# Two-layer diffusion block: adaLN vectors from VectorE to TensorE, beside layer 0's up products

## The chip, the cores and the metric

One core of a Trainium2 chip. The metric is the device time in microseconds of one launch of the whole program, here the median of several runs. All arithmetic is float32, or pairs of reduced-precision float32 parts (below).

## The reference

Two layers work on 256 context tokens and 1024 latent tokens of width 1024. Each layer computes six adaLN vectors, a token mixer and a ConvFFN. Cut to what matters:

```python
def adaln(cv, w, b):
    m = jax.nn.silu(cv) @ w + b                 # cv: (1024,), w: (1024, 6*1024)
    return 6 vectors of 1024: shift, scale, gate of the mixer; shift, scale, gate of the FFN

for i in range(2):
    sh1, sc1, ga1, sh2, sc2, ga2 = adaln(c, w_mod[i], b_mod[i])             # latent tokens
    csh1, csc1, cga1, csh2, csc2, cga2 = adaln(c_ctx, w_mod[i], b_mod[i])   # context tokens
    a = rms_norm(h, g_mix[i]) * (1 + sc1) + sh1
    h = h + ga1 * mixer_i(a)          # layer 0: Fourier mixing and gated linear attention; layer 1: attention
    f = rms_norm(h, g_ffn[i]) * (1 + sc2) + sh2
    h = h + ga2 * conv_ffn(f)         # (silu(conv(f @ w_up)) * ...) @ w_down, width 2 x 2816
```

In layer 1 the context tokens end after the key and value projections, so only its first two vectors (shift and scale of the mixer) are needed for both conditions; the other four are needed for the latent tokens alone.

## The kernel before

Large products run on TensorE in three passes (`mm3`, line 517 on): both operands are split into a high and a low part, and three of the four partial products are summed. Splits are one cast on ScalarE and one subtraction on VectorE or GpSimd (`split`, L207 and L203). All weights and stored activations are loaded by SyncE's queue in the order in which the scheduler puts them.

Both FFN products use a seven-product scheme of block sums. An *up product* of layer 0 is one of seven per half step: 12 matmuls of 320 columns for one 128-wide pair of columns f and one half of the tokens (`up_step`, `PRODS`). There are 22 values of f and two halves: 44 half steps, 308 products. Their results are evacuated by ScalarE (L1306, L1308, L1312, L1316) and added on VectorE, then go through a convolution (`up_conv`, L1332 to L1344) and are stored to `y_d` (L1351). The up weights are loaded by L1216 in pieces of 512 KB, two for each f, and split ahead of time as buffers come free (`Ups`). Seven *down products* follow (`DOWN`, L1460 on: weights loaded by L1447 and L1453, y by L1390). Each has four row blocks of 11 x 2 x 3 matmuls of 320 columns (256 in layer 1). Eleven tiles of y have to be summed and split before each of them (`Ys`); a tile is made when a buffer of `S` is idle, so most of the next product's tiles come while the last row block of the present one runs. L917 adds the results into the residual.

adaLN before is worked on VectorE, apart from the first two vectors of layer 0 (`adaln_pe` has one of them on TensorE). The generator `cond` (L326 to L341) takes a vector in four column quarters of 256. For each quarter and each of eight row chunks k it loads 128 x 256 weights on SyncE's queue (L331, three or five buffers in turn), and multiplies and adds them into an accumulator with one instruction per condition (`nv`): L335 for k = 0, L337 for the others. A 32 x 32 transpose (L340) and a reduction (L341) follow, and at the end of the vector four small matmuls against `sel` (`cond_end`) sum over partitions; each of the four writes its own strip of 32 PSUM partitions. It is called in three places:

- layer 0's vectors 2 to 5, two conditions, in the mixing stage at low priority (lines 986 to 992);
- layer 1's vectors 0 to 3 as the generator `bg` of layer 0's `ffn`, one step at every second f of the down products (L1537 on);
- layer 1's vectors 4 and 5 in the q/k/v stage, two steps for each token chunk (`tok_chunk`, `MODN`).

```python
for v in range(nv):
    a, s = acc[:, v * n:(v + 1) * n], scv[:, k, v:v + 1]
    if k == 0:
        behind(V.tensor_scalar_mul(a, r, s))
    else:
        behind(V.scalar_tensor_tensor(a, r, s, a, ALU.mult, ALU.add))
```

The order on each engine comes from a scheduler that works through the program by priorities; on TensorE, in the FFN, the order is that of the program. Each engine and SyncE's queue then runs its instructions in that order.

Of the kernel before, what the change touches and what calls it, by code (L numbers as in the profile page):

```python
# [20 lines left out]
P = 128  # L21
D = 1024
# [82 lines left out]
def tile_hybrid_dit(  # L105
# [54 lines left out]
    make_identity(nc, ident)  # L160
    V.memset(ones, 1.0)
    V.memset(onesd, 1.0 / D)
    V.tensor_reduce(sel, ident.rearrange("p (q i) -> p i q", i=32), AX.X, ALU.add)
# [83 lines left out]
    with tc.manual_schedule(engines={mybir.EngineType.Activation}):  # L247
        A.activation(scv.rearrange("p k v -> p v k"), vecs[:, 0:16].rearrange("p (v k) -> p v k", v=2), AF.Silu)
        A.preload_act_table_set("natural_log_exp_and_others")
# [24 lines left out]
    def adaln_pe(m, j, raw):  # L274

        ps = psum[:, XB[0] * 512:(XB[0] + 1) * 512]
        for k in range(KT):
            PE.matmul(ps[:2, 0:256], scv[:, k, :], raw[k // 4][:, k % 4, :], start=k == 0, stop=k == KT - 1)
        free(*raw)
        st = SM(256)  # L280
        A.copy(st[:2], ps[:2, 0:256])
        for i in range(2):
            PE.transpose(ps[:, 256 + 2 * i:258 + 2 * i], st[:2, i * P:(i + 1) * P], ident[:2, :2])
        adaln_add(m, j, ps[:, 256:260])

    def adaln_dve(m, j, raw):

        acc = W((2, 256))
        for k in range(KT):
            for v in range(2):  # L290
                if k == 0:
                    V.tensor_scalar_mul(acc[:, v, :], raw[0][:, 0, :], scv[:, 0, v:v + 1])
                else:
                    V.scalar_tensor_tensor(acc[:, v, :], raw[k // 4][:, k % 4, :], scv[:, k, v:v + 1], acc[:, v, :],
                                           ALU.mult, ALU.add)
# [26 lines left out]
    def cond(l, m, nv, n, acc, raw, R, t=None, after=None):  # L322
# [4 lines left out]
        for q in range(D // n):  # L327
            for k in range(KT):
# [3 lines left out]
                for v in range(nv):  # L332
                    a, s = acc[:, v * n:(v + 1) * n], scv[:, k, v:v + 1]
                    if k == 0:
# [651 lines left out]
    with stream(6):  # L986
        ta, tr = AM(1280), AM(1280)
        R = ta[:, 1024:1280].rearrange("p (m v b) -> p m v b", m=4, v=2)
        for m in (2, 3, 4, 5):
            run(cond(0, m, 2, 256, ta[:, 0:512], tr.a, R[:, m - 2], ta[:, 512:1024], start[:, 0:1] if m == 2 else None))  # L990
        cond_end(0, 2, 6, 2, R, XB)
        free(ta, tr)
# [366 lines left out]
    LEAVE = (4, 4, 4, 5, 2, 2, 0)  # L1359
    BGM = 2  # L1360
    AHEAD = 3
# [105 lines left out]

    def ffn(l, n, ups, ops, side, bg, y_d, h_d, after, sides, nsingle, tail, last_groups):

# [10 lines left out]
        for i, (f, hfs) in enumerate(visits):  # L1480
            up = ups.need(i, "A11")
            for hf in hfs:
# [4 lines left out]
                def freed(a, b):  # L1487
# [8 lines left out]
                step = up_step(l, n, hf, f, lambda a: ups.need(i, a), ops[hf], (0, 5) if i < nsingle + 1 else (0, 8) if i < len(visits) - 1 else (0, 4), CU, freed)  # L1496
                while True:
                    try:
# [9 lines left out]
        run(done)  # L1508
        ux.free()
        run(side)  # L1510
# [91 lines left out]
        run(sides)  # L1602
        run(bg)

    def adaln_l1(ms):

        t = S(1280)
        R = halo.rearrange("p f j i -> p (f j i)")
        due = iter(())
        for m in ms:  # L1610
            nv = 2 if m < 2 else 1
            r = R[:, 0:nv * 32].rearrange("p (m v b) -> p m v b", m=1, v=nv)
            for i, _ in enumerate(cond(1, m, nv, 256, t[:, 0:512], t[:, 512:1280], r[:, 0])):
                if i == LATE:
                    next(due, None)
                yield
            due = adaln_end(m, nv, r)
        for _ in range(LATE):
            yield
        next(due, None)  # L1620
        t.free()

    def adaln_end(m, nv, r):
        cond_end(1, m, m + 1, nv, r, (3, 1))
        if m in (1, 4):
            make_gain(1, m // 4)
        yield

    LATE = 6
    h_d = dr.tile([D, TOK], F32, name="h_d")  # L1630
# [100 lines left out]
    with stream(7), tc.manual_schedule(engines={mybir.EngineType.PE}):  # L1731
        def later(): 
            yield from att_side(n_att[0])
        ffn(0, HALF, ups, ops, ffn_side(f_norm[1], ops[1], 1), adaln_l1((0, 1, 2, 3)), y_d, h_d, ffn0_after, later(), 3, a_gen,
            [(r, (0, 1)) for r in range(4)])
# [5 lines left out]

    MODN = 2
    mod_gen = iter(())
# [60 lines left out]
    with stream(8):  # L1804
# [52 lines left out]
        run(a_gen)  # L1857
        mod_gen = adaln_l1((4, 5))
        k_s, v_s = [], []
# [17 lines left out]
    with stream(9.5):  # L1877
        vv(1, v_w())
        free(*a_t[1])
        run(mod_gen)  # L1880

# [246 lines left out]
```

## Time and profile before

| | us |
|---|---|
| three timed runs | 3147.92, 3154.57, 3156.55 (median 3154.57) |
| the profiled execution, and its span | 3148.77, 3147.0 |
| TensorE, VectorE, ScalarE, GpSimd busy | 2786.3, 2548.2, 1446.5, 1529.9 |
| granted clock of TensorE, mean | 0.935 of full |

In the timeline, layer 0's up products run from 713 to 1306 us and its down products to 1690; the q/k/v stage of layer 1 follows. Layer 1's up products run from 2342 to 2860, its down products to 3137. adaLN's L335 and L337 stand from 39 to 331 us (layer 0) and from 1315 to 1806 (layer 1).

How to read it: a line of a group gives program line, engine, operation, tiles, shape and count, then busy us and mean ns of one, then the idle time of the engine ahead of it and what ended that. Lines of waits give who waited for whom: us in total, times, longest. L203 and L207 are helpers (`tt`, `split`) that many stages use; L154 is every matmul.

### The profile page before, as it was taken

What the parts mean: (1) busy time and instruction counts of PE and PEld (TensorE: products, weight loads), DVE (VectorE), ACT (ScalarE), POOL (GpSimd) and SP (SyncE); (2) the same over time, 40 slices, a digit from 0 to 9 for tenths busy, and PEclk for the clock granted to TensorE, in tenths of its full rate; (3) what the DMA queues carried; (4) which work ended last, traced back from release to release, by engine and by line L of the source; (5) the groups of instructions that cost most, each with busy time, mean ns of one, the idle gap of its engine ahead of it and who ended that gap; (6) DMA issues with size and microseconds to landing.
All of it is one profiled execution on the core that took longest, in us unless ns stands there. A gap on an engine that the chain in (4) does not pass through costs nothing.

```text
span 3147.0 us, 52185 instructions
## 1 busy us (share of the span) xinstructions
PE 2786.3 (89%) x19633; PEld 2681.6 (85%) x19633; DVE 2548.2 (81%) x4103; ACT 1446.5 (46%) x2882; POOL 1529.9 (49%) x1229
## 2 busy tenths in 40 slices
PE   6999988987999999976889799999977999888788
PEld 4898977987999999965879788989967899888788
DVE  6899589878778877899987988867768788787774
ACT  3543444545444544422252446756645455454333
POOL 2024284046554444466753563343377665554661
PEclk7999989998999999987899899999988999998899
DMA  8554302421222222696645420030132222228763
GB/s 271 179 171 133 108 31 93 139 100 47 75 72 75 68 77 66 209 282 192 215 137 188 139 82 20 14 97 28 51 99 62 78 76 77 71 65 273 232 218 107
DMA packets 399984, 371.28 MB, mean 118 GB/s; under 512 B 18267, under 2 KB 336371, under 8 KB 399732
## 3 DMA queue, kind: packets, MB, share of 16 engines
q1 hardware_dynamic: 398674, 365.89, 36.8%
q8 instruction: 154, 2.52, 0.3%
q10 hardware_dynamic: 1058, 2.07, 0.2%
q14 instruction: 98, 0.80, 0.1%
HBM read 282.95 MB, written 84.93 MB: 117 GB/s over the span
## 4 chain that ended last, share of the span: by engine, by line
PE 20%; DVE 16%; DMA 5%; issue 5%; ACT 4%; POOL 2%; SPq 0%; DVEq 0%; ACTq 0%; POOLq 0%
PE psum L154 19%; DVE t L203 7%; POOL t L203 2%; DVE t L337 2%; PE psum L158 2%; DMA t<-in_w_ffn_down_dram 1%; DVE t L1777 1%; DMA t<-in_w_mod_dram 1%; ACT t L1332 1%; ACT t L207 1%; DMA t<-in_w_att_out_dram 1%; DVE t L917 1%; DVE ring L203 1%; DVE t L1338 1%; DVE t L1342 1%
## 5 line engine op out<-in xcount | busy, mean ns | idle before, releaser
L154 PE MATMUL psum<-t,t 128*128 128x256 f32 (+3 forms) x17896 | 2614.5, 307 | 280.4 <-DVE t L203 121.4
L154 PEld LDWEIGHTS psum<-t,t 128*128 128x128 f32 x17896 | 2499.0, 197 | 350.4 <-DVE t L203 132.5
L203 POOL TENSOR_TENSOR t<-t,t 128x512 fp32r<-128x512 f32 (+9 forms) x736 | 1068.9, 1467 | 908.7 <-ACT t L207 577.9
L203 DVE TENSOR_TENSOR t<-t,t 128x512 fp32r<-128x512 f32 (+14 forms) x760 | 784.8, 1060 | 146.5 <-ACT t L207 108.9
L207 ACT CAST t<-t 128x512 fp32r<-128x512 f32 (+5 forms) x857 | 555.9, 670 | 706.3 <-POOL t L203 162.9
L203 POOL TENSOR_TENSOR t<-t 128x512 f32<-128x512 f32 (+3 forms) x265 | 328.3, 1255 | 453.1 <-ACT t L663 155.0
L203 DVE TENSOR_TENSOR t<-t,psum 128x320 f32<-128x320 f32 (+4 forms) x416 | 202.1, 506 | 55.8 <-PE psum L154 44.0
L1332 ACT ACTIVATE t<-t,cvs 128x639 f32<-128x639 f32 (+3 forms) x176 | 153.0, 870 | 146.5 <-DVE t L203 137.3
L337 DVE SCALAR_TENSOR_TENSOR t<-t,scv 128x256 f32<-128x256 f32 x224 | 172.8, 797 | 31.1 <-DMA t<-in_w_mod_dram 29.4
L207 ACT CAST t<-psum 128x512 fp32r<-128x512 f32 (+3 forms) x248 | 130.6, 536 | 135.2 <-PE psum L154 57.5
L1926 POOL TENSOR_SCALAR t<-t,ring 128x640 f32<-128x640 f32 x128 | 101.3, 803 | 169.5 <-DVE ring L1916 80.2
L203 DVE TENSOR_TENSOR t<-psum,t 128x512 fp32r<-128x512 f32 (+3 forms) x248 | 151.2, 615 | 35.5 <-ACT t L207 32.7
L158 PE MATMUL psum<-ident,t 128*128 128x128 f32 (+2 forms) x955 | 152.9, 281 | 28.9 <-DVE t L203 17.8
L158 PEld LDWEIGHTS psum<-ident,t 128*128 128x128 f32 (+2 forms) x955 | 113.5, 144 | 38.5 <-DVE t L203 23.3
L1915 DVE TENSOR_REDUCE ring<-psum 128x1 f32<-128x640 f32 x128 | 104.5, 818 | 18.9 <-PE psum L154 13.1
L917 DVE SCALAR_TENSOR_TENSOR t<-psum,mods,t 128x256 f32<-128x256 f32 (+2 forms) x208 | 92.6, 474 | 28.0 <-PE psum L154 26.7
L337 DVE SCALAR_TENSOR_TENSOR t<-t,scv,t 128x256 f32<-128x256 f32 x224 | 112.9, 555 | 2.4 <-DMA t<-in_w_mod_dram 2.1
L1917 ACT ACTIVATE t<-psum,ring 128x640 f32<-128x640 f32 x128 | 102.2, 799 | 21.8 <-DVE ring L1923 9.8
L1337 DVE SCALAR_TENSOR_TENSOR t<-t,cvs 128x641 f32<-128x641 f32 (+1 forms) x44 | 65.0, 1478 | 49.0 <-ACT t L1332 49.0
L1334 ACT ACTIVATE t<-t 128x511 f32<-128x511 f32 (+3 forms) x88 | 60.4, 686 | 75.2 <-DVE t L1338 45.6
L1344 DVE SCALAR_TENSOR_TENSOR t<-t,cvs 128x255 f32<-128x255 f32 (+1 forms) x66 | 90.2, 1390 | 0.6
L1342 DVE SCALAR_TENSOR_TENSOR t<-t,cvs,t 128x255 f32<-128x255 f32 (+1 forms) x66 | 62.4, 971 | 34.9 <-ACT t L1332 34.9
(145 smaller groups left out, 1688.5 us busy)
## 6 DMA issues: line engine op xcount, KB each, us to landing
t<-in_w_ffn_up_dram SPq DMA_DIRECT2D x98, 512.0 KB, 4.1
t<-in_w_mod_dram SPq DMA_DIRECT2D x320, 128.0 KB, 2.6
t<-in_w_ffn_down_dram SPq DMA_DIRECT2D x96, 256.0 KB, 4.3
t<-in_w_even_in_dram SPq DMA_DIRECT2D x28, 512.0 KB, 4.5
t<-in_w_ffn_down_dram SPq DMA_DIRECT2D x72, 192.0 KB, 3.3
t<-y_d SPq DMA_DIRECT2D x20, 640.0 KB, 7.3
t<-in_w_ffn_down_dram SPq DMA_DIRECT2D x24, 512.0 KB, 4.2
t<-in_w_qkv_dram SPq DMA_DIRECT2D x24, 512.0 KB, 4.7
```

What stands on the lines that cost most here:

```text
L154: cls.keep(out_, nc.tensor.matmul(out_, *args, **kw).ins)
L158: cls.keep(out_, nc.tensor.transpose(out_, *args).ins)
L203: return (eng or V).tensor_tensor(out_, a, b, op)
L207: A.copy(hi, src)
L337: behind(V.scalar_tensor_tensor(a, r, s, a, ALU.mult, ALU.add))
L917: last_resid[0] = V.scalar_tensor_tensor(h[:, n % 2, a:b], ps[:, a - c0:b - c0], mods[:, l, m, n, v:v + 1], h[:, n % 2, a:b], ALU.mult, AL ...
L1332: A.activation(x, c[:, j, at:at + m], AF.Identity, bias=tap(l, 3, ft), scale=tap(l, 1, ft))
L1342: V.scalar_tensor_tensor(x[:, s0 + 1:e], c[:, j, 2 + s0:1 + e], tap(l, 0, ft), x[:, s0 + 1:e], ALU.mult, ALU.add)
L1344: i = V.scalar_tensor_tensor(x[:, s0:s1 - 1], c[:, j, 3 + s0:2 + s1], tap(l, 2, ft), x[:, s0:s1 - 1], ALU.mult, ALU.add)
L1915: V.tensor_reduce(mx[:, i:i + 1], ps, AX.XY, ALU.max)
L1917: A.activation(pt[:, i * HALF:(i + 1) * HALF].rearrange("p (b n) -> p b n", b=2), ps, AF.Exp, bias=nb[:, i:i + 1], scale=SCALE, accum_out= ...
L1926: G.tensor_scalar(pt[:, i * HALF:(i + 1) * HALF], pt[:, i * HALF:(i + 1) * HALF], ex[:, i:i + 1], 1.0, ALU.mult, ALU.mult)
```

## The change

Seven vectors leave VectorE: all six of layer 1, and layer 0's last one (5, the gate of the down product). `cond` and `cond_end` stay for layer 0's vectors 2 to 4. The new generator `cond_up` is stepped once after each up product of layer 0, from the second half of the fourth f on. It holds PSUM bank 7 for itself; the up products then turn through seven banks instead of eight. For each of eight chunks k it loads 128 full rows of a vector (512 KB, one buffer in `ring`) and, four products later, issues four float32 matmuls. Their stationary operand is 32 columns of `scv` (the first two are the two conditions; `scv` is padded with zeros for that), the moving one is a column quarter of 256, and each quarter's sums go to its own strip of 32 partitions. The next row's load is issued behind them. After the eighth chunk the sums are copied to SBUF in two pieces (ScalarE); each piece is transposed on TensorE two products after its copy, and one VectorE instruction adds the bias. Both conditions are computed for every vector.

```diff
-    scv = gp.tile([P, KT, 2], F32, name="scv")
+    scv = gp.tile([P, 2 * KT + 32], F32, name="scv")
...
-        for m in (2, 3, 4, 5):
+        for m in (2, 3, 4):
...
-(0, 5) if i < nsingle + 1 else (0, 8) if i < len(visits) - 1 else (0, 4), CU, freed)
+(0, 5) if i < nsingle + 1 else (0, 7) if i < len(visits) - 1 else (0, 4), CU, freed)
...
+                    if hf or i > nsingle:
+                        next(beside, None)
...
-                    if f % BGM:
-                        next(bg, None)
...
+    def cond_up(vecs_lm, bank):
+        ps = psum[:, bank * 512:(bank + 1) * 512]
+        raw, st = ring[:, 0:D], ring[:, D:D + P]
+        for l, m in vecs_lm:
+            for k in range(KT):
+                DMA(raw, w_mod[l, k * P:(k + 1) * P, m * D:(m + 1) * D])
+                for _ in range(COND_LATE):
+                    yield
+                for g in range(4):
+                    PE.matmul(ps[g * 32:(g + 1) * 32, 0:256], scv[:, 2 * k:2 * k + 32], raw[:, g * 256:(g + 1) * 256],
+                              start=k == 0, stop=k == KT - 1)
+            for i in range(2):
+                A.copy(st, ps[:, i * P:(i + 1) * P])
+                yield
+                yield
+                PE.transpose(ps[:, 256 + i * P:256 + (i + 1) * P], st, ident)
+            sums = ps[:, 256:512].rearrange("p (i g q) -> p g i q", i=2, q=32)[:, :, :, 0:2]
+            tt(mods[:, l, m].rearrange("p (g i) v -> p g i v", i=2), sums,
+               bmod(l, m).rearrange("p (g i) v -> p g i v", i=2), ALU.add)
+            if l and m in (1, 4):
+                make_gain(1, m // 4)
+    COND_LATE = 4
...
-        ffn(0, ..., adaln_l1((0, 1, 2, 3)), ...)
+        ffn(0, ..., cond_up([(1, 0), (1, 1), (0, 5)] + [(1, m) for m in (2, 3, 4, 5)], 7), ...)
...
-        for _ in range(MODN):
-            next(mod_gen, None)
...
-        mod_gen = adaln_l1((4, 5))
...
-        run(mod_gen)
```

The order on TensorE in the middle of layer 0's up products, before: two rows of six matmuls are one product (the names are the weight tile and the tile of the tokens' operand).

```order
L154 MATMUL psum<-t_6132,t_8528 128x320 x6
L154 MATMUL psum<-t_6135,t_8528 128x320 x6
L154 MATMUL psum<-t_6172,t_8546 128x320 x6
L154 MATMUL psum<-t_6252,t_8546 128x320 x6
L154 MATMUL psum<-t_6167,t_8549 128x320 x6
L154 MATMUL psum<-t_6247,t_8549 128x320 x6
```

The same engine at such a place now, from one group of adaLN matmuls to the next:

```order
L154 MATMUL psum<-ring,scv 32x256 x4
L154 MATMUL psum<-t_6602,t_9078 128x320 x6
L154 MATMUL psum<-t_6680,t_9078 128x320 x6
L154 MATMUL psum<-t_6641,t_9081 128x320 x6
L154 MATMUL psum<-t_6739,t_9081 128x320 x6
L154 MATMUL psum<-t_6660,t_9101 128x320 x6
L154 MATMUL psum<-t_6720,t_9101 128x320 x6
L154 MATMUL psum<-t_5904,t_9274 128x320 x6
L154 MATMUL psum<-t_5951,t_9274 128x320 x6
L154 MATMUL psum<-ring,scv 32x256 x4
```

Four float32 matmuls of 256 columns stand between every fourth and fifth product, 56 times, and two transposes after each eighth time.

VectorE in layer 0's down products, between the second and the third of them, before (t of 128 x 640 are splits of y, of 128 x 1280 sums of y; `ring,mods` are residual adds):

```order
L917 SCALAR_TENSOR_TENSOR t_12503<-ring,mods,t_12503 128x320
L203 TENSOR_TENSOR t_12737<-t_11759,t_12737 128x640
L337 SCALAR_TENSOR_TENSOR t_11815<-t_11815,scv 128x256 x2
L203 TENSOR_TENSOR t_12765<-t_11759,t_12765 128x640
L203 TENSOR_TENSOR t_11786<-t_12681,t_11786 128x1280
L203 TENSOR_TENSOR mods<-psum,vecs 128x16
L337 SCALAR_TENSOR_TENSOR t_11815<-t_11815,scv 128x256 x4
L203 TENSOR_TENSOR t_12853<-t_11786,t_12853 128x640
```

And now, at the same seam:

```order
L918 SCALAR_TENSOR_TENSOR t_12629<-ring,mods,t_12629 128x320
L204 TENSOR_TENSOR t_12837<-t_11973,t_12837 128x640
L204 TENSOR_TENSOR t_12000<-t_12778,t_12000 128x1280
L204 TENSOR_TENSOR t_12869<-t_12000,t_12869 128x640
L204 TENSOR_TENSOR t_12317<-t_12799,t_12317 128x640
L204 TENSOR_TENSOR t_12873<-t_12317,t_12873 128x640
```

The adaLN instructions between splits, sums and adds are gone; nothing stands in their place. (The changed program's lines lie one higher from line 162 on.)

SyncE's queue in the middle of the up products, before, over two values of f:

```order
L1216 DMA t_10991<-in_w_ffn_up_dram 128x8x128
L1216 DMA t_10975<-in_w_ffn_up_dram 128x8x128
L1351 DMA y_d<-t_6310 128x641
L1351 DMA y_d<-t_6310 128x639
L1216 DMA t_11231<-in_w_ffn_up_dram 128x8x128
L1216 DMA t_11215<-in_w_ffn_up_dram 128x8x128
```

And now:

```order
L1217 DMA t_10410<-in_w_ffn_up_dram 128x8x128
L1217 DMA t_10394<-in_w_ffn_up_dram 128x8x128
L1611 DMA ring<-in_w_mod_dram 128x1024
L1352 DMA y_d<-t_6207 128x641
L1611 DMA ring<-in_w_mod_dram 128x1024 x2
L1352 DMA y_d<-t_6207 128x639
L1217 DMA t_10665<-in_w_ffn_up_dram 128x8x128
L1611 DMA ring<-in_w_mod_dram 128x1024
L1217 DMA t_10649<-in_w_ffn_up_dram 128x8x128
```

The rows of adaLN weights stand among the up weights and the stores of y, some right behind both up loads of an f, some between them.

More of the change, by code (lines that the diff above doesn't have):

```diff
@@ L161, in tile_hybrid_dit @@
     V.memset(ones, 1.0)
+    V.memset(scv, 0.0)
     V.memset(onesd, 1.0 / D)
@@ L247, in tile_hybrid_dit @@
     with tc.manual_schedule(engines={mybir.EngineType.Activation}):
-        A.activation(scv.rearrange("p k v -> p v k"), vecs[:, 0:16].rearrange("p (v k) -> p v k", v=2), AF.Silu)
+        A.activation(scv[:, 0:2 * KT].rearrange("p (k v) -> p v k", v=2), vecs[:, 0:16].rearrange("p (v k) -> p v k", v=2), AF.Silu)
         A.preload_act_table_set("natural_log_exp_and_others")
@@ L277, in adaln_pe @@
         for k in range(KT):
-            PE.matmul(ps[:2, 0:256], scv[:, k, :], raw[k // 4][:, k % 4, :], start=k == 0, stop=k == KT - 1)
+            PE.matmul(ps[:2, 0:256], scv[:, 2 * k:2 * k + 2], raw[k // 4][:, k % 4, :], start=k == 0, stop=k == KT - 1)
         free(*raw)
@@ L291, in adaln_dve @@
                 if k == 0:
-                    V.tensor_scalar_mul(acc[:, v, :], raw[0][:, 0, :], scv[:, 0, v:v + 1])
+                    V.tensor_scalar_mul(acc[:, v, :], raw[0][:, 0, :], scv[:, v:v + 1])
                 else:
-                    V.scalar_tensor_tensor(acc[:, v, :], raw[k // 4][:, k % 4, :], scv[:, k, v:v + 1], acc[:, v, :],
+                    V.scalar_tensor_tensor(acc[:, v, :], raw[k // 4][:, k % 4, :], scv[:, 2 * k + v:2 * k + v + 1], acc[:, v, :],
                                            ALU.mult, ALU.add)
@@ L332, in cond @@
                 for v in range(nv):
-                    a, s = acc[:, v * n:(v + 1) * n], scv[:, k, v:v + 1]
+                    a, s = acc[:, v * n:(v + 1) * n], scv[:, 2 * k + v:2 * k + v + 1]
                     if k == 0:
@@ L1359, in tile_hybrid_dit @@
     LEAVE = (4, 4, 4, 5, 2, 2, 0)
-    BGM = 2
     AHEAD = 3
@@ L1466, in tile_hybrid_dit, with ffn @@
     WE = ((G, G, G), (V, G, V))
-    def ffn(l, n, ups, ops, side, bg, y_d, h_d, after, sides, nsingle, tail, last_groups):
+    def ffn(l, n, ups, ops, side, beside, y_d, h_d, after, sides, nsingle, tail, last_groups):
         u = n // 2
@@ L1495, in freed @@
                         pump(w_gen, (W, 1))
-                step = up_step(l, n, hf, f, lambda a: ups.need(i, a), ops[hf], (0, 5) if i < nsingle + 1 else (0, 8) if i < len(visits) - 1 else (0, 4), CU, freed)
+                step = up_step(l, n, hf, f, lambda a: ups.need(i, a), ops[hf], (0, 5) if i < nsingle + 1 else (0, 7) if i < len(visits) - 1 else (0, 4), CU, freed)
                 while True:
@@ L1508, in ffn @@
         run(done)
+        run(beside)
         ux.free()
@@ L1602, in ffn @@
         run(sides)
[L1603 to L1615, printed above, removed]
-                yield
[L1617 to L1629, printed above, removed]
+    def cond_up(vecs_lm, bank):
[11 more added lines that the diff above has]
+                A.copy(st, ps[:, i * P:(i + 1) * P])
+                yield
+                yield
[6 more added lines that the diff above has]
+    COND_LATE = 4
     h_d = dr.tile([D, TOK], F32, name="h_d")
@@ L1733, in later @@
             yield from att_side(n_att[0])
-        ffn(0, HALF, ups, ops, ffn_side(f_norm[1], ops[1], 1), adaln_l1((0, 1, 2, 3)), y_d, h_d, ffn0_after, later(), 3, a_gen,
+        ffn(0, HALF, ups, ops, ffn_side(f_norm[1], ops[1], 1), cond_up([(1, 0), (1, 1), (0, 5)] + [(1, m) for m in (2, 3, 4, 5)], 7), y_d, h_d, ffn0_after, later(), 3, a_gen,
             [(r, (0, 1)) for r in range(4)])
```

6 lines of the change are left out of this document (2 added, 4 removed).

## The prediction

> **What bounds the kernel now.** I read the stages first. These windows are layer 0's up products (two parts: start and steady run), its down products, the first part of layer 1's q/k/v stage, and layer 1's down products. The borders come from the timeline: the last evacuation of an up product and the last residual add of a stage. Columns: us, then busy us (instructions) of each engine, granted clock, DMA share, GB/s.
>
> ```profile
> 713.00:830.00 117.00, 96.66 (x569) 94.11 (x568) 96.51 (x116) 62.26 (x104) 74.83 (x52) 0.87 0.19 58
> 830.00:1260.00 430.00, 425.97 (x2895) 424.77 (x2895) 344.32 (x433) 211.94 (x370) 211.17 (x183) 1.00 0.23 72
> 1306.00:1690.00 384.00, 306.74 (x1880) 296.04 (x1879) 356.66 (x467) 118.11 (x197) 230.05 (x155) 0.88 0.69 214
> 1690.00:1860.00 170.00, 138.77 (x1063) 133.16 (x1061) 149.10 (x317) 74.01 (x238) 95.53 (x87) 0.91 0.37 114
> 2860.00:3137.00 277.00, 243.84 (x1911) 238.69 (x1910) 190.35 (x279) 95.94 (x179) 140.53 (x97) 0.92 0.66 207
> ```
>
> The steady up run is TensorE's: 425.97 of 430 us busy at full clock. Whatever TensorE is given there lengthens the span one for one. Layer 0's down stage is VectorE's: 356.66 of 384 us, while TensorE has 306.74 and a clock of 0.88. In layer 1's down stage, which has no adaLN beside it, VectorE is busy 190.35 of 277 us.
>
> What does TensorE need there by itself? The code gives 7 products x 4 row blocks x 11 x 2 halves x 3 = 1848 matmuls per down stage. The next two windows lie in runs without a gap, of 320 columns (layer 0) and of 256 (layer 1):
>
> ```profile
> 1000.00:1100.00 100.00, 100.00 (x683) 100.00 (x682) 80.64 (x101) 49.05 (x86) 46.66 (x42) 1.00 0.22 69
> 2966.00:2986.00 20.00, 20.00 (x171) 20.00 (x170) 10.72 (x15) 5.88 (x11) 12.21 (x10) 1.00 0.74 220
> ```
>
> So one matmul takes 0.146 us at 320 columns and 0.117 us at 256. Layer 0's down stage needs 1848 x 0.146 = 270 us and takes 384: it loses 114. Layer 1's needs 216 us, and some 7 for the 64 final transposes (at 0.11 us, an estimate from the 0.216 us per 256 float32 columns found below), and takes 277: it loses 54.
>
> Who makes TensorE wait in layer 0's down stage, who holds the DMA queue, and what the chain of waits goes through (three views of 1306 to 1690):
>
> ```profile
> PE psum L154 <- DVE t L203: 51.9, 18, 10.0
> PE psum L154 <- ACT t L207: 11.3, 7, 5.8
> PE psum L154 <- POOL t L203: 7.2, 4, 2.6
> SPq L331 <- DVE t L337: 98.5, 82, 4.8
> SPq L331 <- DVE t L335: 30.4, 17, 5.8
> by line: DVE t L203 13.0%; DVE t L337 9.9%; DMA t<-in_w_mod_dram 8.3%; issue 6.5%; DVE t L917 4.5%; DMA t<-in_w_ffn_down_dram 1.1%; DMA t<-sd 1.0%; DVE t L335 1.0%; DVE ring L340 0.7%; ACT t L207 0.5%; SPq L331 0.5%; POOL t L203 0.3%; DVE h
> ```
>
> TensorE waits for VectorE's splits of y, at the seams between products. VectorE has adaLN instructions (L335, L337) between those splits, and SyncE's queue stands 129 us behind them with its next adaLN row, so that weight and y loads behind it come late too. adaLN's own part of the chain is 9.9 + 8.3 + 1.0 + 0.7 + 0.5 = 20.4% of 384 = 78 us.
>
> **The change, part by part.**
>
> *Down stage, layer 0: removed.* adaLN's instructions there:
>
> ```profile
> L337 DVE SCALAR_TENSOR_TENSOR t<-t,scv 128x256 f32<-128x256 f32 x176 | 136.7, 809 | 19.3 <-DMA t<-in_w_mod_dram 18.3
> L335 DVE TENSOR_SCALAR t<-t,scv 128x256 f32<-128x256 f32 x26 | 18.1, 722 | 1.2 <-DMA t<-in_w_mod_dram 1.1
> L340 DVE STREAM_TRANSPOSE ring<-t 128x512 f32<-128x512 f32 (+1 forms) x16 | 9.2, 574 | 0.3
> L341 DVE TENSOR_REDUCE halo<-ring 128x16 f32<-128x512 f32 (+1 forms) x15 | 8.4, 558 | 0.4
> ```
>
> That is 172 of VectorE's 357 busy us, and all L331 transfers with their queue waits. What remains is late next: the y splits, sums and residual adds of VectorE (185 us), GpSimd's splits (230 us), TensorE's 270. Three prices for the gain. Low: adaLN's share of VectorE, 172/357, of the 52 us for which TensorE sat behind it: 25 us. Nearest row: layer 1's loss of 54 us, scaled by 320/256 since y is wider, is 67; 114 - 67 = 47 us. High: adaLN's part of the chain, 78 us. I take 52: layer 1 is the nearest, and it carries weight splits on VectorE that layer 0 leaves to GpSimd. The freed buffer (one more y tile made ahead) is within that.
>
> *q/k/v stage: removed.* Two vectors with one condition each:
>
> ```profile
> L337 DVE SCALAR_TENSOR_TENSOR t<-t,scv 128x256 f32<-128x256 f32 x48 | 36.2, 754 | 11.8 <-DMA t<-in_w_mod_dram 11.2
> L335 DVE TENSOR_SCALAR t<-t,scv 128x256 f32<-128x256 f32 x6 | 4.0, 672 | 0.0
> PE psum L158 <- DVE t L203: 15.7, 6, 5.2
> PE psum L154 <- DVE halo L341: 5.2, 1, 5.2
> by line: DVE t L1777 19.1%; DVE t L203 17.4%; PE psum L154 15.0%; issue 14.8%; DVE t L337 9.2%; DVE ring L203 5.2%; DMA t<-in_w_qkv_dram 4.8%; DMA t<-in_w_mod_dram 3.7%; DVE ring L1123 1.8%; DVE t L335 1.6%; DVE ring L340 1.2%; DVE ring L38
> ```
>
> The chain carries 9.2 + 3.7 + 1.6 + 1.2 = 15.7% of 170 = 27 us of adaLN. TensorE's waits behind VectorE are 21 us, of which the 5.2 for adaLN's own reduction surely goes, and of the others adaLN's 40 of 149 busy us: 9 us. Between 9 and 27 I take 17.
>
> *Mixing stage: removed.* A quarter of the vectors there (one of four, two conditions):
>
> ```profile
> L337 DVE SCALAR_TENSOR_TENSOR t<-t,scv,t 128x256 f32<-128x256 f32 x202 | 103.0, 563 | 1.4 <-DMA t<-in_w_mod_dram 1.3
> PE psum L154 <- DVE t L203: 21.6, 17, 3.1
> PE psum L154 <- DVE cvs L238: 5.1, 2, 4.3
> ```
>
> 56 of L337's instructions at 0.563 are 32 us of VectorE, between 100 and 350 us. TensorE waits for VectorE only later (350 to 720: the last two rows), 27 us. The scheduler also orders the GLA and Fourier work anew, which can cost as well as gain. I take a gain of 6, between -8 and 20.
>
> *Up stage, layer 0: added.* 7 vectors x 8 chunks = 56 bursts of four float32 matmuls of 256 columns, to four strips of 32 partitions. No row has such a burst. One strip alone (8 matmuls, two passes each) is in the first row; then four strips at 8, 16 and 64 columns. At 8 columns, 1640.18 starts the first pass and 1640.24 the second, with the products before and after beside them; at 16 and 64 columns the two rows are the two passes:
>
> ```profile
> 75.79 3.62 PE L154 MATMUL psum<-t,scv 128*2 128x256 f32 x16
> 1639.94 0.31 PE L154 MATMUL psum<-t,t 128*128 128x320 f32 x1
> 1640.18 0.25 PE L154 MATMUL psum<-halo,sel 128*32 128x8 f32 x8
> 1640.62 0.60 PE L154 MATMUL psum<-t,t 128*128 128x320 f32 x3
> 1640.24 0.19 PE L154 MATMUL psum<-halo,sel 128*32 128x8 f32 x3
> 1527.30 0.20 PE L154 MATMUL psum<-halo,sel 128*32 128x16 f32 x1
> 1527.35 0.21 PE L154 MATMUL psum<-halo,sel 128*32 128x16 f32 x4
> 406.97 0.30 PE L154 MATMUL psum<-t,sel 128*32 128x64 f32 x4
> 407.07 0.31 PE L154 MATMUL psum<-t,sel 128*32 128x64 f32 x4
> ```
>
> A pass of 256 columns in one strip takes about 3.46/16 = 0.216 us (3.62 less the last one's tail). The 8-column burst cost the stream of products 1640.62 - 1639.94 - 2 x 0.146 = 0.39 us, with a pass of 0.05 to 0.06. At 16 columns a pass is still 0.05, at 64 it is 0.10: twice what one strip of 64 would take by the first row (64 x 0.216/256 = 0.054). If four strips run fully beside each other, a burst is 0.39 + 2 x (0.216 - 0.055) = 0.71 us, 40 us for all. If the 0.10 grows with the columns, a pass is 0.40 and a burst 1.08, 60 us. One after another: eight passes of 0.216 and the switching, about 2.0 us, 112 in all. The 64-column row is nearest in size, so I take 1.0: 56 us. The 14 transposes are 128 columns each with a switch: an estimate from the same row is 0.11 for the columns and as much for the gap: 3 us. The copies, the seven adds and the gains lie beside products on engines with room (ScalarE 212, VectorE 344 of 430 us). One PSUM bank fewer costs nothing: a half step uses four, and seven still leave each one nearly a whole step before its next use.
>
> *New waits.* One row buffer: after a burst the next 512 KB row has four products, 48 x 0.146 = 7.0 us, to land. SyncE's queue is in order, and in it stand the up weights and the y stores (window 830 to 1260):
>
> ```profile
> SPq L1216 <- POOL t L203: 98.0, 16, 6.9
> SPq L1351 <- DVE t L203: 255.4, 34, 13.9
> t<-in_w_ffn_up_dram SPq DMA_DIRECT2D x98, 512.0 KB, 4.1
> ```
>
> An equal transfer lands in 4.1 us, so 2.9 are spare. Every second up load waits 98.0/16 = 6.1 us for GpSimd. Where a row stands right behind one, its burst and all products behind it on TensorE wait. In the order about eight rows stand so, most of them nearly ready; I take 3 us, between 0 and 60.
>
> **Sum.** Gains 52 + 17 + 6 = 75, costs 56 + 3 + 3 = 62: 13 us less. The profiled run took 3148.8 us (span 3147.0), the median of the three timed is 3154.6, 5.8 above it; the same step from the median gives 3142 us.
>
> **Rivals.**
> - *Bursts fully parallel.* 0.71 us each, and no late row: 16 + 3 us better, and with the down stage's gain nearer the chain's, 65, 32 better in all: 3110. For it: 8 and 16 columns cost the same. Against: 0.10 at 64. The Trainium skill, "TensorE: Matmul & The Clock Gate", Part 3, says that matmuls to different 32-column strips run concurrently, with about 4 ns for each more; by that a burst would be about 0.7 us. By that rule the trace agrees up to 16 columns, not at 64.
> - *GpSimd takes over the down stage.* Its 230 us have to go into a shorter stage, and it waits for casts and loads. Then the gains are the low ones, 25 + 9, 35 less than I took: 22 slower, 3177. For it: its waits are short in TensorE's list (7.2 us), but VectorE stood ahead of them. Against: 230 us are still less than TensorE's 270. It decides once the down stage's gain is under 39 us.
> - *Late rows.* SyncE stands at an up load waiting for GpSimd while a row behind it is due. At 3 us for each of some 18 visits, 54: 51 more than I took, 38 slower, 3193. It decides from 16 us of late rows in all.
> - *Strips one after another.* 112 us for 56: 43 slower, 3198. It decides from 1.23 us a burst. Against it: four strips of 64 in 0.10 us instead of 0.22. The Trainium skill, "TensorEngine Tiling (Array Packing)", Key Properties, adds that changing the tiling mode drains TensorE; the measured 0.39 us holds that.
>
> That the change does not do what it says is excluded by the order: the bursts stand among the products.
>
> **Chances.** Forecast 0.50, parallel bursts 0.20, GpSimd 0.14, late rows 0.09, serial strips 0.07. Within the forecast the unknown burst price (40 to 60) and the down gain (25 to 78) spread it some 25 us either way, so it holds both signs: its own range is 3118 to 3168. About 0.3%, 9 us, is what a measurement can tell. Faster: 0.58 of the forecast and the parallel case, 0.49. Within: a quarter of the forecast and 0.045 of GpSimd's, 0.17. Slower: the rest, 0.34. The range 3098 to 3192 reaches past the parallel case and up to the late rows; it leaves out the serial strips and the tails, under 0.2.
>
> **What would show it.** Right: the steady up run grows by about 14% with TensorE still full; four strips' passes 0.3 to 0.4 us apart; the down stage at about 332 us with VectorE near 60%; the waits of L331 gone; 1690 to 1860 some 17 shorter. Wrong: TensorE idle ahead of a burst with the row's DMA as releaser (late rows); GpSimd as releaser at the seams; bursts of 0.7 or 2 us.

## The result and the profile after

The changed kernel takes 3109.64 us (median of 6 runs, 3100.83 to 3113.73) against 3158.82 us (median of 6, 3147.92 to 3162.15) for the kernel before on the same chip: ratio 0.9845, 95% interval 0.9824 to 0.9866. It is 49 us faster. The prediction had 13 us faster, and a range of 3098 to 3192 that holds the time. The profiled runs are 3148.77 and 3111.55 us (spans 3147.0 and 3109.8), 37 us apart; the profiled run of before was one of its quicker ones.

Line numbers of the changed kernel are one higher than before in the parts named here (L203 is now L204, L917 now L918, L706 now L707). The stages below are cut at the first ScalarE copy of an up product (L1306, now L1307), the last one (L1316, now L1317), and the last residual add of the down products (L917, now L918).

| stage, us in the profiled runs | before | after | difference | forecast |
|---|---|---|---|---|
| mixing, to the start of up | 712.8 | 725.6 | +12.8 | -6 |
| up products of layer 0 | 591.9 | 627.0 | +35.1 | +62 |
| down products of layer 0 | 387.2 | 322.6 | -64.6 | -52 |
| q/k/v and attention, to up of layer 1 | 649.9 | 625.8 | -24.1 | -17 |
| FFN of layer 1 | 805.1 | 808.8 | +3.7 | 0 |
| sum | 3147.0 | 3109.8 | -37.2 | -13 |

Each stage length comes from one profile. How far such a length moves by itself is seen in the FFN of layer 1, whose work no edit of this document changes: it takes 794.0 to 815.0 us in the thirteen profiled kernels.

The windows of the changed kernel that answer to those of the prediction: start and steady part of up, down, the first part of q/k/v, and layer 1's down products (us, then busy us and instructions of TensorE, its weight loads, VectorE, ScalarE, GpSimd, then granted clock, DMA share, GB/s):

```profile
726.00:843.00 117.00, 96.58 (x596) 91.65 (x595) 94.79 (x113) 60.74 (x102) 74.22 (x53) 0.88 0.27 81
843.00:1310.00 467.00, 466.90 (x3329) 435.00 (x3328) 326.04 (x440) 214.26 (x381) 213.53 (x181) 1.00 0.39 124
1354.00:1675.00 321.00, 291.99 (x1859) 286.73 (x1859) 217.29 (x231) 120.26 (x198) 236.78 (x155) 0.93 0.64 199
1675.00:1845.00 170.00, 152.16 (x1214) 149.08 (x1212) 129.92 (x284) 83.70 (x280) 105.92 (x100) 0.95 0.27 86
2820.00:3100.00 280.00, 246.22 (x1940) 241.12 (x1939) 192.01 (x282) 96.83 (x180) 141.37 (x97) 0.93 0.67 209
```

The steady up run is full: 466.90 of 467 us, where before it had 425.97 of 430. The down stage has lost VectorE's adaLN (356.66 to 217.29 us of work), TensorE is 91% busy in it in place of 80%, and its granted clock rose from 0.88 to 0.93. Who TensorE waits for there now (the list of waits from 1354 to 1675: us, times, longest):

```profile
PE psum L154 <- DVE t L204: 13.9, 6, 5.4
PE psum L154 <- POOL t L204: 7.8, 7, 3.2
PE psum L154 <- DVE t L918: 3.8, 1, 3.8
```

51.9 us behind VectorE's splits have become 13.9. GpSimd is next in the list, with 7.8 us where it had 7.2: it did not take over.

VectorE's busy time fell by 139 us, less than the strips' 172. The other 231 instructions are the same in both, but the sums of y, which read SBUF alone, now take longer, while the adds from PSUM do not (first before, then after, in the down stage):

```profile
L203 DVE TENSOR_TENSOR t<-t,t 128x1280 f32<-128x1280 f32 x19 | 31.9, 1680 | 0.0
L917 DVE SCALAR_TENSOR_TENSOR t<-psum,mods,t 128x320 f32<-128x320 f32 x38 | 19.7, 541 | 0.2 <-PE psum L154 0.2
L204 DVE TENSOR_TENSOR t<-t,t 128x1280 f32<-128x1280 f32 x19 | 39.2, 2069 | 0.0
L918 DVE SCALAR_TENSOR_TENSOR t<-psum,mods,t 128x320 f32<-128x320 f32 x39 | 20.0, 542 | 29.9 <-PE psum L154 21.4 <-ACT t L1566 8.5
```

Over all of the 231, those that read SBUF alone went from 1.21 to 1.40 us on average, those that read PSUM stayed at 0.51; together they are busy for 217 us where it was 196, and VectorE for 68% of the stage, not near 60%. GpSimd's share of the stage rose from 60% to 74% beside them; whether that is the reason was not tested.

In up, SyncE's queue waits for TensorE before most rows, because the one row buffer must be read first, and a row lands 4.0 us after its issue (median of 56). Two of the queue's waits from 843 to 1300, and a line of the list of DMA issues:

```profile
SPq L1611 <- PE psum L154: 112.5, 42, 9.6
SPq L1217 <- POOL t L204: 59.5, 18, 6.6
```

```profile
ring<-in_w_mod_dram SPq DMA_DIRECT2D x56, 512.0 KB, 4.0
```

No burst was late: by the records, TensorE waited ahead of none of the 56.

### The profile page after: what moved, and what is told of

Read it like the earlier page. It is cut to its first block, busy times and chain, and to the rows that moved or that the text cites. A ratio compares the mean times of both kernels' runs of the same rounds, so it can differ in the third digit from the quotient of the medians.

```text
span 3109.8 us, 52191 instructions
## 1 busy us (share of the span) xinstructions
PE 2812.2 (90%) x20047; PEld 2680.2 (86%) x20047; DVE 2332.2 (75%) x3729; ACT 1448.9 (47%) x2896; POOL 1535.5 (49%) x1229
## 5 line engine op out<-in xcount | busy, mean ns | idle before, releaser
L154 PE MATMUL psum<-t,t 128*128 128x256 f32 (+4 forms) x17896 | 2615.2, 306 | 208.2 <-DVE t L204 77.5
L204 POOL TENSOR_TENSOR t<-t,t 128x512 fp32r<-128x512 f32 (+8 forms) x736 | 1077.6, 1479 | 866.1 <-ACT t L208 523.3
L204 DVE TENSOR_TENSOR t<-t,t 128x512 fp32r<-128x512 f32 (+13 forms) x760 | 808.8, 1092 | 168.3 <-ACT t L208 123.6
L204 POOL TENSOR_TENSOR t<-t 128x512 f32<-128x512 f32 (+3 forms) x265 | 327.7, 1254 | 390.4 <-ACT t L664 157.4
L204 DVE TENSOR_TENSOR t<-t,psum 128x320 f32<-128x320 f32 (+4 forms) x416 | 202.9, 508 | 126.4 <-PE psum L154 94.3
L208 ACT CAST t<-psum 128x512 fp32r<-128x512 f32 (+4 forms) x248 | 130.7, 536 | 134.2 <-PE psum L158 60.0
L204 DVE TENSOR_TENSOR t<-psum,t 128x512 fp32r<-128x512 f32 (+4 forms) x248 | 151.3, 615 | 37.0 <-ACT t L208 33.9
L918 DVE SCALAR_TENSOR_TENSOR t<-psum,mods,t 128x256 f32<-128x256 f32 (+2 forms) x208 | 91.9, 473 | 62.7 <-PE psum L154 53.2
L204 DVE TENSOR_TENSOR ring<-ring 128x1 f32<-128x1 f32 (+5 forms) x296 | 76.2, 259 | 20.8 <-ACT ring L1912 12.8
L1313 ACT COPY t<-psum 128x320 f32<-128x320 f32 (+1 forms) x88 | 35.2, 400 | 121.2 <-PE psum L154 121.2
L1338 DVE SCALAR_TENSOR_TENSOR t<-t,cvs 128x641 f32<-128x641 f32 (+1 forms) x44 | 52.0, 1182 | 47.3 <-ACT t L1333 47.3
L1343 DVE SCALAR_TENSOR_TENSOR t<-t,cvs 128x255 f32<-128x255 f32 (+1 forms) x66 | 53.7, 840 | 44.5 <-ACT t L1333 44.5
L338 DVE SCALAR_TENSOR_TENSOR t<-t,scv,t 128x256 f32<-128x256 f32 x168 | 80.1, 527 | 3.1 <-DMA t<-in_w_mod_dram 2.9
```

What stands on the lines that cost most here:

```text
L154: cls.keep(out_, nc.tensor.matmul(out_, *args, **kw).ins)
L204: return (eng or V).tensor_tensor(out_, a, b, op)
L208: A.copy(hi, src)
L918: last_resid[0] = V.scalar_tensor_tensor(h[:, n % 2, a:b], ps[:, a - c0:b - c0], mods[:, l, m, n, v:v + 1], h[:, n % 2, a:b], ALU.mult, AL ...
L1343: V.scalar_tensor_tensor(x[:, s0 + 1:e], c[:, j, 2 + s0:1 + e], tap(l, 0, ft), x[:, s0 + 1:e], ALU.mult, ALU.add)
```

## The experiments

All were timed in alternation with the kernel before, so each has its own ratio to it. Stage lengths are cut as above.

### Are the four strips worked beside each other?

The burst in the changed kernel, on TensorE's timeline (start us, us, operation, count): eight records are four products of two passes each.

```profile
1033.62 0.46 PE L154 MATMUL psum<-t,t 128*128 128x320 f32 x2
1034.01 0.64 PE L154 MATMUL psum<-ring,scv 128*32 128x256 f32 x8
1034.58 0.85 PE L154 MATMUL psum<-t,t 128*128 128x320 f32 x4
```

In the records of this and of the other 55 bursts the first passes of the four strips start at 0, 7, 13 and 20 ns, the second passes at 240, 247, 253 and 260, within a nanosecond or two, and the next up matmul 0.31 us after the last of them. From starts of up matmuls on both sides, less their usual spacing of 0.147 us, a burst costs 0.77 us; the 56 together cost 42.9. To see what the strips are worth, all four products went to the same 32 columns:

```diff
-PE.matmul(ps[g * 32:(g + 1) * 32, 0:256], ..., start=k == 0, stop=k == KT - 1)
+PE.matmul(ps[0:32, 0:256], ..., start=k == 0 and g == 0, stop=k == KT - 1 and g == 3)
```

> The changed kernel with all four products of a burst on partitions 0 to 31 of the PSUM bank, so on the same 32 columns of the array, as one accumulation; so the four quarters of a vector are summed into one, and three quarters of the values are left out. Theory A (the four products run beside each other only because they sit on four column strips): six passes more of 0.21 to 0.24 us in a burst, 1.3 to 1.45 us; 56 bursts cost 72 to 81 us more, up takes about 700 us in place of 627, the median is about 3183 us. Theory B (the burst is cheap because each product is short, wherever it lies): no burst changes, and the median stays at 3110 us, within 0.3%.

Measured: 3174.30 us, ratio 1.0055 (1.0035 to 1.0074). A burst of that kernel on the timeline:

```profile
1037.71 1.19 PE L154 MATMUL psum<-t,t 128*128 128x320 f32 x7
1038.83 1.92 PE L154 MATMUL psum<-ring,scv 128*32 128x256 f32 x8
1040.67 1.59 PE L154 MATMUL psum<-t,t 128*128 128x320 f32 x9
```

The eight passes now start 216 ns apart (the first two 240), and a burst costs 2.04 us; up takes 695.5 us, 68 more. So theory A holds: side by side on four strips, four products take the time of one. The change would have been 17 us slower than before without it.

### How near are the rows to being late?

```diff
-    COND_LATE = 4
+    COND_LATE = 2
```

> The changed kernel with the row's products two up products after its load was issued, not four: some 3.5 us in place of 7 (an up product takes about 1.75 us) for a row that landed in 4.0 us (median) in the changed kernel. Transposes are two products behind their copy as before. Theory A (TensorE is in order and waits for a late row with all up products behind it): a wait of about 0.5 to 1 us ahead of most bursts, 30 to 55 us in up, the median at 3140 to 3165 us. Theory B (a row is issued far enough ahead in time even so, because the issuing queue runs ahead of TensorE): no wait at the bursts, the median within 0.3% of 3110 us.

Measured: 3134.11 us, ratio 0.9944 (0.9914 to 0.9975), up 658.8 us, 32 more than in the changed kernel. TensorE's waits from 840 to 1370:

```profile
PE psum L154 <- DMA ring<-in_w_mod_dram: 21.9, 18, 2.6
PE psum L154 <- DVE t L204: 5.2, 2, 2.7
```

Theory A holds: TensorE stands for the late row. The list counts 18 waits; by the starts of the matmuls, 38 of the 56 bursts begin over 0.03 us late, the latest by 2.7 us, and all together by 28 us. The median is a little below what theory A gave. With four products in between none begins late.

### What made the down stage 64 us shorter?

The kernel before, with parts of the strips taken out of layer 0's down products. First the loads alone:

```diff
-                DMA(r, src[:, k, q * n:(q + 1) * n])
+                if l == 0 or q * KT + k < raw.shape[1] // n:
+                    DMA(r, src[:, k, q * n:(q + 1) * n])
```

> The kernel before, without the loads of layer 1's adaLN strips but for the first three of each vector: VectorE's multiply-adds stay, on rows that are already there, so layer 1's adaLN is computed from the wrong rows. No transfer of 0.13 MB takes its place in the queues. Theory A (the down stage lost its time to VectorE, which has these strips in front of the h1 splits and evictions that TensorE waits for): down stays at 375 to 385 us, and the median is 3150 to 3158 us. Theory B (it lost it to the loads, in front of the y loads in SP's queue or in the DMA engines): down falls to about 325 to 335 us, and the median to about 3100.

Three loads of each vector stay. Then the multiply-adds alone:

```diff
-                    else:
+                    elif l == 0:
                         behind(V.scalar_tensor_tensor(a, r, s, a, ALU.mult, ALU.add))
```

> The kernel before, with the loads of layer 1's adaLN strips kept, but without 7 of 8 of their multiply-adds on VectorE (the first row of each sum is taken alone, so layer 1's adaLN is one row's product, not the sum). Theory A (VectorE's work): down falls from 385 to about 325 us, the q, k, v stretch loses some 15 to 25 us as well, and the median is about 3075 to 3090 us, lower than the changed kernel's 3110, since no burst is paid in up. Theory B (the loads): down stays above 375 us, the median at 3145 to 3158 us. In between, the two share it, by their parts.

As the two did not add up to the whole, both edits together, and then the strips left out altogether (`iter(())` in place of `adaln_l1((0, 1, 2, 3))`, with `mods` and `gains` set to zero). The first three kernels lack the same parts in layer 1's vectors 4 and 5, in q/k/v, so their whole times hold more than the down stage; the fourth keeps these two vectors.

> The kernel before, with both left out among the down products: layer 1's adaLN loads (but for three of each vector) and 7 of 8 of their multiply-adds on VectorE; the strips' transposes, reductions, products with the selector and the evictions of the sums stay, so layer 1's adaLN is one row's product. The loads alone were worth 9 us of the down stage, the multiply-adds alone 33; the change took 64 off it. Theory A (the two hold the same waits, so that either keeps part of what the other would give): down falls to about 325 us, 62 less, and the median is 3075 to 3085. Theory B (they add up, 9 + 33, and the other 22 us come from what follows the strips, the transposes, reductions and selector products): down is about 345 us, and the median 3090 to 3098.

> The kernel before without layer 1's adaLN of vectors 0 to 3 among the down products, loads, VectorE and TensorE parts alike (these four vectors stay at zero; 4 and 5 are computed among the q, k and v products as before). Both theories of the 64 us as the work of these strips in one form or another: down is 318 to 325 us, as in the changed kernel, up 592, and the median is 3075 to 3085 us. Rival: part of the 64 us came from elsewhere (what the bursts in up change in the order of what is pumped ahead into the down stage): then down stays above 335 us.

The down stage's window in each (loads out; multiply-adds out; both out; nothing left):

```profile
1301.00:1679.00 378.00, 307.47 (x1895) 296.22 (x1894) 355.59 (x472) 120.94 (x200) 237.99 (x156) 0.86 0.56 175
```

```profile
1298.00:1653.00 355.00, 301.13 (x1906) 292.34 (x1905) 241.44 (x294) 119.42 (x199) 234.35 (x156) 0.90 0.75 233
```

```profile
1303.00:1641.00 338.00, 295.64 (x1893) 288.46 (x1891) 243.99 (x292) 120.64 (x199) 232.28 (x156) 0.92 0.63 196
```

```profile
1302.00:1626.00 324.00, 290.88 (x1860) 285.12 (x1860) 219.52 (x232) 120.53 (x199) 237.67 (x156) 0.93 0.64 199
```

| left out | down, us | less than before | TensorE's wait for VectorE's splits | whole kernel, us | ratio to before |
|---|---|---|---|---|---|
| nothing (before) | 387.2 | | 51.9 | 3154 to 3158 | 1 |
| loads | 377.8 | 9 | 48.0 | 3135.61 | 0.9932 (0.9908 to 0.9957) |
| 7 of 8 multiply-adds | 354.1 | 33 | 21.8 | 3103.56 | 0.9834 (0.9802 to 0.9866) |
| both | 338.1 | 49 | 23.5 | 3082.43 | 0.9761 (0.9738 to 0.9784) |
| the strips altogether | 324.2 | 63 | 13.9 | 3080.26 | 0.9743 (0.9713 to 0.9773) |
| the change itself | 322.6 | 65 | 13.9 | 3109.64 | 0.9845 (0.9824 to 0.9866) |

VectorE's work is the largest part, but neither pure theory is right: with the loads left and most multiply-adds gone, the DMA share is still 0.75 and the stage is 31 us longer than in the change. Loads and multiply-adds together are worth 49, more than the 9 + 33 of each alone, so 7 us were held by either. The last 14 us belong to what stayed in the third kernel: the transposes, reductions, selector products and first multiplications, 24 us of VectorE by the two windows (243.99 - 219.52), twelve loads, and the buffer of `S` that the strips hold, which without them can take one more tile of y. No run tells these apart. So neither of the theories on the sum holds either: the truth lies between their 325 and 345 us. That the strips explain all of it, with the buffer that they hold, is shown by the last kernel: 324.2 us without any burst in up.

### What made q/k/v shorter?

Layer 1's vectors 4 and 5 back among the q, k and v products:

```diff
...
-cond_up([(1, 0), (1, 1), (0, 5)] + [(1, m) for m in (2, 3, 4, 5)], 7)
+cond_up([(1, 0), (1, 1), (0, 5)] + [(1, m) for m in (2, 3)], 7)
...
+        for _ in range(MODN):
+            next(mod_gen, None)
...
+        mod_gen = adaln_l1((4, 5))
...
```

> The changed kernel with layer 1's vectors 4 and 5 back on VectorE among the q, k and v products, as in the kernel before; 40 bursts in place of 56. Theory A (the 25 us that the stretch from the end of the down stage to up of layer 1 gained come from the strips of these two vectors): that stretch takes about 650 us in place of 626, up is 12 us shorter, the median is about 3122 us. Theory B (the 25 us come from the down stage handing over its queues and buffers earlier, not from these strips): the stretch stays at about 626 to 630 us, up is 12 us shorter, the median is about 3098 to 3102 us.

Measured: 3121.17 us, ratio 0.9886 (0.9854 to 0.9918). The stretch from down to the next up, before, in the changed kernel, and in this one:

```profile
1692.00:2342.00 650.00, 583.48 (x4153) 548.53 (x4152) 510.12 (x1222) 357.48 (x885) 303.03 (x289) 0.96 0.22 70
```

```profile
1675.00:2301.00 626.00, 579.53 (x4143) 545.66 (x4142) 479.75 (x1151) 356.92 (x884) 299.58 (x287) 0.97 0.19 61
```

```profile
1661.00:2304.00 643.00, 583.15 (x4155) 549.07 (x4155) 514.75 (x1233) 356.88 (x884) 300.87 (x287) 0.96 0.23 72
```

Mostly theory A: 17 of the 24 us are the two vectors' strips, and the bursts saved in up were 9.5 us. The other 7 stay gained with the strips back, so they are not theirs, and their cause stays open. A down stage that ends sooner does not give them by itself: the kernel without strips in the down stage has the two vectors' strips here too, and its stretch takes 655.7 us, 6 more than before. Nor are 7 us clear of the spread: in the seven profiled kernels with all of layer 1's vectors in up, this stretch takes 622 to 633 us.

### Why did the mixing stage become longer?

VectorE has 30 us less to do there, and the stage took 13 us more. Whole stage and its second half, before and after:

```profile
0.00:713.00 713.00, 624.36 (x4288) 582.25 (x4289) 591.54 (x1028) 311.56 (x595) 243.63 (x198) 0.91 0.42 135
350.00:713.00 363.00, 319.73 (x2225) 305.42 (x2224) 287.86 (x500) 166.63 (x362) 149.27 (x119) 0.92 0.27 92
```

```profile
0.00:726.00 726.00, 627.46 (x4272) 583.74 (x4273) 561.47 (x958) 311.44 (x597) 243.02 (x199) 0.90 0.39 127
350.00:726.00 376.00, 319.81 (x2116) 303.42 (x2115) 287.96 (x496) 163.07 (x358) 148.93 (x120) 0.88 0.26 87
```

At 350 us the changed kernel is ahead: it has 2116 matmuls of this stage left where the kernel before had 2225. But they keep TensorE busy as long (319.81 and 319.73 us), at a granted clock of 0.88 in place of 0.92, and TensorE is idle for 56 us in place of 43. So the time is lost behind 350 us, where no strip stands in either kernel (the last is at 331 us before, at 253 after). First, layer 0's vector 5 put back:

```diff
...
-        for m in (2, 3, 4):
+        for m in (2, 3, 4, 5):
...
-cond_up([(1, 0), (1, 1), (0, 5)] + [(1, m) for m in (2, 3, 4, 5)], 7)
+cond_up([(1, m) for m in (0, 1, 2, 3, 4, 5)], 7)
```

> The changed kernel, but layer 0's vector 5 (the down gate) stays on VectorE in the mixing stage, as in the kernel before; only layer 1's six vectors go through TensorE, 48 bursts in place of 56. In the changed kernel up began at 725.6 us against 712.8 before, though VectorE had less to do there. Theory A (taking vector 5's strips out of the mixing stage lets other work of that stage come in another order, and this costs the 13 us): up begins at about 713 us, up is shorter by 8 bursts of 0.77 us, 6 us, the down stage keeps its 322 us, and the profiled span is 3109.8 - 13 - 6, about 3091 us. Theory B (the 13 us have another cause, the other shape of the condition's tile or a lower granted clock in that run, and the strips themselves cost time in this stage, as the prediction had it with 6 us): up begins at 726 to 732 us and the span is 3104 to 3110 us.

Measured: 3087.58 us, ratio 0.9778 (0.9751 to 0.9805), which is faster than the changed kernel, too. Its mixing, up and down:

```profile
0.00:710.00 710.00, 619.09 (x4293) 577.81 (x4293) 592.44 (x1029) 311.90 (x596) 244.62 (x198) 0.92 0.42 136
...
710.00:1331.00 621.00, 592.52 (x4080) 559.73 (x4081) 457.90 (x596) 301.24 (x525) 307.48 (x249) 0.98 0.36 115
1331.00:1651.00 320.00, 288.90 (x1865) 283.09 (x1864) 217.48 (x232) 120.76 (x200) 240.53 (x156) 0.94 0.64 201
```

Up begins at 709.5 us, the span is 3088.6 against the 3091 that theory A gave. So the removal of vector 5 from this stage is what costs. The other kernels fall in the same two groups: up begins at 711 to 713 us in the four that keep this stage as before (the down-stage tests), and at 723 to 728 in the three that keep it as changed (one strip, rows two products ahead, q/k/v). Next, is it an unlucky order of its two large parts? In the changed kernel the gated linear attention (GLA) came earlier and Fourier later than with vector 5 in it: GLA's last mask copy at 508 us against 516, Fourier's last eviction at 582 against 566. Fourier's priority was raised:

```diff
-    with stream(4):
+    with stream(0.5):
         FM = S.sub(5)
         fourier(W, FM)
```

> The changed kernel with the Fourier part of the mixing stage placed ahead of the GLA part in the scheduler's order (its stream's number is 0.5 in place of 4); nothing else. In the changed kernel the GLA steps came some 10 us earlier than with vector 5's strips among them, and the Fourier steps 7 to 15 us later (its last evictions at 552 us against 545), and the out products, which need Fourier's result, began 17 us later. Theory A (the 13 us are the scheduler's order, in which GLA takes the slots that the strips leave, and Fourier, which the out products wait for, is pushed back): Fourier's last eviction comes at 545 us or before, the out products' first residual before 575, up begins at 695 to 715 us, and the median is 3085 to 3100. Theory B (the order of the two doesn't matter, GLA and Fourier together have to be done before up): up begins at 722 to 735 us and the median is 3105 to 3120.

Measured: 3108.17 us, ratio 0.9842 (0.9810 to 0.9874); up begins at 721.7. This didn't test what it was to test: GLA's last mask copy moved from 508 to 519 us, but Fourier's last eviction stayed at 582. Theory A's numbers did not come, and the number of the stream does not set the order by itself. The cleaner test adds work and takes none away: vector 5's strips come back as idle work without loads, while TensorE still computes the vector in up. Then the same with half of the strips:

```diff
-                DMA(r, src[:, k, q * n:(q + 1) * n])
+                if m < 5:
+                    DMA(r, src[:, k, q * n:(q + 1) * n])
...
-        for m in (2, 3, 4):
+        for m in (2, 3, 4, 5):
...
```

> The changed kernel, with vector 5's strips back on VectorE in the mixing stage as idle work: 64 multiply-adds, transposes and reductions on rows that already lie there, without the 32 loads; TensorE computes the vector in up as in the changed kernel and overwrites the result. So it has all the work of the changed kernel and 50 us of VectorE work more. Theory A (the scheduler's order of the whole mixing stage follows from what VectorE is given there, and the order without vector 5 is worse by 13 to 16 us): up begins at 708 to 715 us, 11 to 17 us sooner in spite of the added work, and the median is 3092 to 3098 us. Theory B (the loads of vector 5, not its work, held the other order in place): up begins at 724 to 730 us, the median is 3108 to 3115. A third value, above 730 or between 716 and 723, would say that the stage takes another length with each change in its work list, with no simple cause.

```diff
-        for q in range(D // n):
+        for q in range(D // n if m < 5 else 2):
...
```

> As the kernel with vector 5's strips as idle work, but only two of its four strips (32 multiply-adds, no loads). Theory A: the order comes back with half the work too, up begins at 708 to 715 us; Theory B: 724 to 730. If the stage's length jumps with every change of its work list, it is neither, and it need not lie between 710 and 726 either.

Measured: all strips 3089.57 us, ratio 0.9785 (0.9753 to 0.9818); half of them 3107.25, ratio 0.9847 (0.9808 to 0.9886). Whole mixing stage of the one and of the other:

```profile
0.00:712.00 712.00, 622.12 (x4290) 580.22 (x4291) 593.58 (x1028) 312.00 (x594) 245.27 (x198) 0.92 0.40 129
```

```profile
0.00:725.00 725.00, 629.02 (x4282) 585.61 (x4283) 577.34 (x991) 311.02 (x593) 242.53 (x198) 0.90 0.39 127
```

With 32 us of useless VectorE work more than the changed kernel (593.58 to 561.47; the expectation's 50 was too high) the stage is 14 us shorter. More work for an engine does not explain a shorter stage, so the order is what is left, and the loads are not needed for it. With half of the work (16 us) it stays long, which theory A did not give. Of TensorE's waits, the one that differs most is that for L707 (L706 before, L708 in the kernels with idle strips), which copies GLA's masked products from PSUM on VectorE. The lines for the second half of the stage, in this order: before, in the changed kernel, with vector 5 put back, with all idle strips, with half of them, with Fourier's priority raised:

```profile
PE psum L154 <- DVE t L706: 1.5, 1, 1.5
```

```profile
PE psum L154 <- DVE t L707: 11.7, 8, 4.1
```

```profile
PE psum L154 <- DVE t L707: 1.5, 1, 1.5
```

```profile
PE psum L154 <- DVE t L708: 0.6, 1, 0.6
```

```profile
PE psum L154 <- DVE t L708: 12.3, 6, 4.4
```

```profile
PE psum L154 <- DVE t L707: 7.6, 4, 5.3
```

In the kernels whose up begins at 709 to 713 us this wait is 0.6 to 1.5 us; in those where it begins at 722 to 728 it is 7.6 to 12.3. The granted clock behind 350 us goes with it: 0.91 to 0.92 in the first group, 0.87 to 0.89 in the second. Which of the two is a cause, and which a companion, was not tested.

## Why the prediction was right in direction and wrong in size

- **Burst, the term that failed first.** "The 64-column row is nearest in size, so I take 1.0: 56 us." A burst costs 0.77 us, 43 in all: a pass of four strips takes 0.24, not 0.40. The 0.10 us at 64 columns did not grow in proportion to the columns; on one strip the first pass of a burst takes 0.24 as well. The two bounds were good: 0.71 for strips side by side, 2.0 for one after another, where one strip gave 2.04. The Trainium skill, "TensorE: Matmul & The Clock Gate", Part 3, has matmuls on different strips run concurrently, some 4 ns apart; here they start 7 ns apart. By that rule the rival "bursts fully parallel" stood at 3110, which is where the time came out; the row that I let speak against it was two passes of a shape four times smaller, and in that row, too, the trace has the four strips start 6 or 7 ns apart. That the time came out at this figure is partly luck: the rival's sum, too, had the mixing stage 19 us too short, and it missed some 15 us of gains in up and q/k/v.
- **Late rows and transposes.** 3 us each; there was no late row, and from the starts of the up matmuls around them a transpose costs 0.11 us, 1.5 us for the 14.
- **Up gave some back.** The bursts' 42.9 us made up only 35 us longer. TensorE's idle time fell: from 4.0 us in the 430 us of the steady window to 0.1 in 467, and in all of up from 31 to 25. The remaining 2 or 3 us are not explained.
- **Down stage.** Taken 52, measured 65, within the bounds of 25 and 78. The step that failed is scaling layer 1's loss by 320/256, to 67 us. What layer 0 loses now is 322.6 - 270 = 53 us, close to layer 1's 54 as it stands. That VectorE's work was the main cause was right; the loads' share was in it, too. The 185 us for "the y splits, sums and residual adds of VectorE" were too few: these instructions were busy for 196 us before and for 217 after.
- **q/k/v.** The strips there were priced at 17 us and are worth 17. The other 7 us of the stretch were not in the sum, and their cause is open.
- **Mixing, wrong in sign.** "I take a gain of 6, between -8 and 20"; it cost 13, outside the bounds. The text named the new order of GLA and Fourier as a risk, but priced the removed work. The work was hidden, and the new order cost more than it: with the strips back as idle work, up begins at 712 us again.
- **Rivals.** GpSimd's takeover would have shown in TensorE's waits: 7.8 us where 7.2 had been. Serial strips and late rows would both have been real: at one strip the kernel is slower than before, and rows issued two products ahead cost 24 us of median.

In sum, against the forecast in the profiled runs: bursts and the rest of up 27 us better, down 13 better, q/k/v 7 better, mixing 19 worse, layer 1 4 worse: 24 us, from -13 to -37.

## What to carry to other kernels

Small products with 32 outputs belong on four column strips at once: four float32 products of 256 columns cost TensorE 0.77 us beside a stream of larger ones, and 2.04 us on one strip. Take work away from a stage that VectorE bounds (63 us here), but before moving work out of a stage where it is hidden, ask what the scheduler does with the gap: leaving layer 0's gate in the mixing stage makes this kernel 3088 us in place of 3110. Where a stage with less to do becomes longer, put the work back as idle work: this tells an order from a cost.

## What the runs showed of the hardware that was not expected

- Four strips start 7 ns apart, the second pass of all four 0.24 us after the first. Of the 0.77 us of a burst, some 0.3 are the change of shape at its two ends (0.77 less two passes of 0.24), and only 0.48 the products. The Trainium skill, "TensorEngine Tiling (Array Packing)", Key Properties, says that a change of tiling mode drains TensorE, and gives no time for it; the 0.3 us are what such a change in and out can have cost here at most.
- In the down stage, VectorE's instructions that read SBUF alone take 1.21 us on average before, and still in the kernel without loads; 1.31 in the kernel without most multiply-adds, and 1.40 in the changed kernel. Those that read PSUM stay at 0.51.
- On one strip the passes of 256 float32 columns follow each other every 216 ns, the duration that the sixteen passes at 75.79 us had in the kernel before.
- In the steady up run the granted clock stays at 1.00 with the bursts in it; in the down stage it rose with TensorE's share, from 0.88 at 80% to 0.93 at 91%.
